# A hybrid RWKV, gMLP and expert block on one core: norm, modulation and gather edits, and the reversed values moved behind the receptance products

## The chip, the core and the metric

The kernel runs on one core of a Trainium2 chip. The core has a matrix engine (TensorE, PE in the profile), a vector engine (VectorE, DVE), a scalar engine (ScalarE, ACT) and a general engine (GpSimd, POOL), each with its own instruction stream; SyncE (SP) issues the DMAs. The engines share the on-chip memory (SBUF) and PE's accumulation banks (PSUM) and wait for each other on semaphores. The metric is the device time of one execution in microseconds (us), the median of several.

## The reference, cut to what matters

One layer over 512 latent and 256 context tokens, width 1024, float32:

```python
h = layer_norm(x) * (1 + sc1) + sh1          # context likewise
z = h @ w_in                                 # rwkv 3*1024 + 384, sgu 2*1024, gates 2*1024
# branch A: RWKV-7, forward and reverse
r, k, v, decays, kk, a = rwkv_prep(centred_shift(z_rwkv))
y_f, y_b = rwkv_scan(..., reverse=False), rwkv_scan(..., reverse=True)
bonus = sum(r * k * r_k, -1, keepdims=True) * v
y_a = (group_norm(y_f + y_b) * lnx_g + lnx_b + bonus) * g
# branch B: gating over chunks of 128 positions, 8 groups
u, v = split(gelu(z_sgu), 2)
v = layer_norm(v, sgu_ln_g, sgu_ln_b)
v = einsum('gpq,bnqgc->bnpgc', sgu_w, v) + sgu_b
y_s = u * v
x = layer_norm(ALPHA*x + gt1 * (merged(y_a, y_s) @ w_out), ln1_g, ln1_b)
# experts: 16, each takes its 64 best tokens
h = layer_norm(x) * (1 + sc2) + sh2
gate, idx = top_k(softmax(h @ router_w), 64)
ye = (silu(h[idx] @ w1) * (h[idx] @ w3)) @ w2 * gate
x = layer_norm(ALPHA*x + gt2 * segment_sum(ye, idx), ln2_g, ln2_b)
```

## The kernel before

The kernel is one program whose stages follow each other: loads, norm and transposes (to 50 us), the RWKV projections (to 316), the values of the gating branch (to 362), the gating branch and gates, with the preparation of the scan woven in (to 583), the scan (to 880), readout, output product and output norm (to 1004), router and top-k (to 1043), and the experts.

Projections. Every weight block is split into a high part `H` (ACT, line 159) and a rest `L` (line 160, on POOL or DVE) and PE multiplies with both: `zl` are products for the latent tokens, `zc` for the context. A loop runs over eight channel tiles `ct`, and its code is written by hand in the order in which each engine is to run it (`manual_schedule`). An iteration has the products for the keys (`z_k`, in two halves), the small products `b<-xp,wp` of decay and rate (`prep_a`, direction 0 or 1), the receptance (`z_r`) and the values (`z_v`). `shift_in` makes the shifted rows `kt`, `rt`, `vt` out of them: ACT starts each (line 351) and DVE adds two neighbours (lines 353 and 355, twice for a tile that has context). `prep_scan` on DVE is `g` (line 435) and a scan (line 437), then exponentials on ACT (442 to 444). `prep_vr` makes `vr` on ACT, the values with each 128 columns reversed; `prep_v` transposes `vt` and `vr` on PE (line 512) and copies the results to `vs` on ACT (line 513); `prep_bonus` is a product `bon<-rk,bones` on PE and `bo` on DVE (line 521). These three treat the tile of the iteration before (`ct - 1`).

The second tile of decay inputs, `pair_x`, is a copy of `dw` or `da` (ACT `xp`), its rest (DVE `xl`) and a DMA to the other half of the partitions.

Gating branch. Units run in a written list; `u` and `a`, `s`, `b` are products of the gating and gate columns. Ahead of them DVE normalises four tiles `vg` (line 1042), multiplies by the scale row and adds the bias row (lines 1043 and 1044). `ada_part` adds up the modulation (`adacc`, DVE line 567) and `ada_row` turns it into a row with products `adr` on PE.

Experts. `h2` is the normalised stream; POOL multiplies and adds the modulation rows (lines 1282 and 1283). The router does not read these but has the modulation in its columns. `gather` picks the tokens of two experts by products with one-hot columns `oh` and copies them to `xe` on ACT. The expert weights `we` come through 16 buffers.

## Time and profile before

| | us |
|---|---|
| median of three runs | 1998.64 (1995.78 to 1999.15) |
| the profiled execution | 1992.99 |
| its span, first to last instruction | 1991.0 |
| PE busy in the span | 1768.8 (89%) |
| DVE busy | 924.9 (46%) |
| ACT busy | 589.9 (30%) |
| POOL busy | 260.5 (13%) |

The busy times are those of the profiled execution, on one core, and add up stages with different limits. The profile's columns: a group of rows of a timeline gives the start, the busy time, the engine, the line of the kernel, the operation, the tiles written and read, how many instructions the row joins, and in brackets the idle time before it and what ended that.

### The profile page before, as it was taken

The page shows a single profiled execution, that of the slowest core. Times are in us where ns is not written, and L with a number is a line of the kernel's source. Part 1 is how long each engine was busy: PE and PEld are TensorE (multiplying, and loading weights), DVE is VectorE, ACT ScalarE, POOL GpSimd, SP SyncE. Part 2 cuts the span into 40 slices and gives each one's busy share as a digit, 9 for nine tenths or more (in the row PEclk, how much of TensorE's full clock was granted, in tenths as well). Part 3 has the DMA queues.
Part 4 walks back from the last instruction along what each step waited for, and adds up shares of the span by engine and source line. Part 5 has one row for each costly group of instructions (what it writes and reads, how often), then busy time and mean ns, then how long its engine had stood idle before and what let it go on. Part 6 is the DMA issues. An engine that isn't in the chain of part 4 may idle for free.

```text
span 1991.0 us, 32397 instructions
## 1 busy us (share of the span) xinstructions
PE 1768.8 (89%) x13248; PEld 1130.4 (57%) x13248; DVE 924.9 (46%) x1681; ACT 589.9 (30%) x1009; POOL 260.5 (13%) x207
## 2 busy tenths in 40 slices
PE   6999999899997979788959999899998899999895
PEld 3877778687777878677844434334343333434324
DVE  6689886688837768876970020010102002020115
ACT  2676775243246555343221111001011001011101
POOL 4422234010020100055520000000000000000000
PEclk9999999899999989898959999999999999999998
DMA  9365557567697667593289999999999999999995
GB/s 329 98 194 161 172 185 228 169 217 231 218 270 170 155 151 181 113 289 127 75 338 373 426 426 427 426 427 427 426 427 426 427 427 427 426 426 427 426 421 208
DMA packets 364011, 592.41 MB, mean 298 GB/s; under 512 B 220372, under 2 KB 282068, under 8 KB 315736
## 3 DMA queue, kind: packets, MB, share of 16 engines
q1 hardware_dynamic: 363864, 590.35, 80.3%
q8 instruction: 105, 1.72, 0.3%
q14 instruction: 42, 0.34, 0.1%
HBM read 541.78 MB, written 47.71 MB: 296 GB/s over the span
## 4 chain that ended last, share of the span: by engine, by line
DMA 41%; PE 8%; DVE 5%; issue 1%; POOL 0%; ACT 0%; DVEq 0%; SPq 0%; POOLq 0%; ACTq 0%
DMA we<-in_e 41%; PE hh L74 3%; PE yx L74 1%; PE co L74 1%; PE ye L74 1%; DVE x L1258 1%; PE lg L74 1%; PE xe L74 0%; DMA w<-in_wba 0%; DVE mt L1200 0%; DVE x L1266 0%; DVE mgL L1204 0%; PE hT L1518 0%; DVE wk L1436 0%; DVE m L1435 0%
## 5 line engine op out<-in xcount | busy, mean ns | idle before, releaser
L74 PE MATMUL hh<-we,xe 128*64 128x512 f32 x2048 | 462.3, 596 | 24.9 <-DMA we<-in_e 24.9
L74 PEld LDWEIGHTS hh<-we,xe 128*64 128x64 f32 x2048 | 149.5, 137 | 323.6 <-issue 261.0
L74 PE MATMUL ye<-we,hidT 128*64 128x512 f32 (+1 forms) x1216 | 254.0, 533 | 37.2 <-DMA we<-in_e 36.9
L1508 DVE TENSOR_TENSOR hd<-hd,hh 64x512 f32<-64x512 f32 x64 | 44.2, 690 | 518.7 <-ACT hd L1507 517.7
L74 PE MATMUL zl<-hL,H 128*128 128x512 f32 x816 | 261.6, 402 | 1.1 <-DVE hf L319 1.1
L74 PEld LDWEIGHTS ye<-we,hidT 128*64 128x64 f32 x1216 | 83.1, 136 | 200.1 <-DMA we<-in_e 105.3
L1507 ACT ACTIVATE hd<-hh 64x512 f32<-64x512 f32 x64 | 37.8, 590 | 490.9 <-PE hh L74 490.9
L74 PEld LDWEIGHTS zl<-hL,H 128*128 128x128 f32 x816 | 155.8, 193 | 30.2 <-issue 2.8
L74 PE MATMUL zl<-hL,L 128*128 128x512 f32 x408 | 163.5, 401 | 9.8 <-DVE L L160 9.8
L160 POOL TENSOR_TENSOR L<-w,H 128x1024 fp32r<-128x1024 f32 x54 | 138.4, 2571 | 206.0 <-ACT H L159 145.4
L1601 POOL TENSOR_TENSOR x<-x,row 128x1024 f32<-128x1024 f32 x2 | 4.6, 2338 | 941.5 <-DVE rv L129 941.5
L159 ACT ACTIVATE H<-w 128x1024 fp32r<-128x1024 f32 x91 | 94.9, 1053 | 87.2 <-PE zl L74 27.7
L1526 ACT ACTIVATE ye<-ye 64x512 f32<-64x512 f32 (+1 forms) x34 | 18.8, 553 | 271.5 <-PE ye L74 271.2
L1527 DVE SCALAR_TENSOR_TENSOR ye<-ye,gate,srow 64x512 f32<-64x512 f32 (+1 forms) x38 | 23.9, 664 | 147.7 <-ACT ye L1526 147.4
L74 PEld LDWEIGHTS zl<-hL,L 128*128 128x128 f32 x408 | 78.8, 193 | 21.8 <-DVE L L160 10.8
L716 DVE TENSOR_TENSOR tmpi<-Dt,Xt 128x31 f32<-128x31 f32 (+15 forms) x186 | 63.6, 342 | 14.6 <-DMA Dt<-Asd 8.9
L718 DVE TENSOR_TENSOR Xt<-Xt,tmpi 128x31 f32<-128x31 f32 (+15 forms) x186 | 63.8, 343 | 6.5
L74 PEld LDWEIGHTS xe<-oh,h 128*128 128x128 f32 x512 | 59.6, 196 | 8.9 <-issue 8.9
L74 PE MATMUL co<-ye,ohT 128*128 128x512 f32 (+1 forms) x144 | 62.7, 591 | 0.0
L74 PE MATMUL xe<-oh,h 128*128 128x128 f32 x512 | 61.8, 282 | 0.7 <-DVE oh L1459 0.7
L74 PEld LDWEIGHTS zc<-hC,H 128*128 128x128 f32 x288 | 54.0, 188 | 12.7 <-POOL hC L321 0.4
L160 DVE TENSOR_TENSOR L<-w,H 128x1024 fp32r<-128x1024 f32 x37 | 46.1, 1245 | 30.3 <-ACT H L159 28.7
(327 smaller groups left out, 2889.3 us busy)
## 6 DMA issues: line engine op xcount, KB each, us to landing
we<-in_e SPq DMA_DIRECT2D x376, 1024.0 KB, 19.6
w<-in_w_ch SPq DMA_DIRECT2D x51, 512.0 KB, 5.0
w<-in_ada_w SPq DMA_DIRECT2D x32, 512.0 KB, 5.3
xx<-Xkd SPq DMA_DIRECT2D x28, 512.0 KB, 5.6
adaw<-in_ada_w SPq DMA_DIRECT2D x16, 512.0 KB, 10.3
we<-in_e SPq DMA_DIRECT2D x32, 256.0 KB, 5.5
Xkd<-g SPq DMA_DIRECT2D x32, 192.0 KB, 2.7
Ald<-al SPq DMA_DIRECT2D x16, 384.0 KB, 2.3
```

The costliest lines, as they stand in the source:

```text
L74: PE.matmul(o, l, r, start=start, stop=stop, skip_group_check=True)
L159: S.activation(h, t, AF.Copy)
L160: (eng or G).tensor_tensor(l, t, h.bitcast(F32), OP.subtract)
L716: V.tensor_tensor(tv, Dt[:, j, None, j + 1:].to_broadcast([128, m, n]), X[:, 0:m, j:j + 1].to_broadcast([128, m, n]), OP.mult)
L718: V.tensor_tensor(X[:, 0:m, j + 1:], X[:, 0:m, j + 1:], tv, OP.subtract)
L1258: V.scalar_tensor_tensor(t[:, hs], R["x", i][:, hs], ALPHA, t[:, hs], op0=OP.mult, op1=OP.add)
L1507: S.activation(hd, pn[n][0:64], AF.Silu)
L1508: V.tensor_tensor(hd, hd, pn[n][64:128], OP.mult)
L1526: S.activation(y, p, AF.Copy)
L1527: V.scalar_tensor_tensor(y, p if same else y, gv[e - j][rs], gt2[rs, cs], op0=OP.mult, op1=OP.mult)
L1601: G.tensor_tensor(acc[i], acc[i], l2[0], OP.mult)
```

## The change

Five parts. `pair_x` makes tiles for the latent and the context columns apart (`xp`, `xl` and `xc`), with two copies where there was one. In the projection loop the copy `vr`, its transposes and copies, and the bonus product with `bo` stand around `z_r` in place of ahead of `prep_a`; the transposes of `vt` stay. In the gating branch the scale and bias of the norm are no longer applied to `vg`: the scale goes into the operation behind the product, and the bias into a tile `sbt` made of the sums of the gating weights (two products `cs`). `ada_row` is run once three more weight blocks have been split. The modulation of `h2` on POOL is gone, and `gather` applies it in its copies, one for each 128 columns. The diff, without the tables of columns and rows on the host's side and the reuse of a small tile:

```diff
@@ -292,16 +292,17 @@
             V.tensor_tensor(w[h], t[h], w[h].bitcast(F32), OP.subtract)
 
     def pair_x(t):
+        A, B = (T([128, 2, TL], n, F32R) for n in ("xp", "xl"))
+        Cc = T([128, 4, TC], "xc", F32R)
         hs = []
         for d in range(2):
             h, o = slice(64 * d, 64 * d + 64), slice(64 - 64 * d, 128 - 64 * d)
-            x2 = T([128, TT], "xp", F32R)
-            S.activation(x2[h], t[h], AF.Copy)
-            SY.dma_start(x2[o].bitcast(F32), x2[h].bitcast(F32))
-            lo = T([128, TT], "xl", F32R)
-            G.memset(lo[o].bitcast(F32), 0.0)
-            V.tensor_tensor(lo[h], t[h], x2[h].bitcast(F32), OP.subtract)
-            hs.append((x2, lo))
+            for x2, lo, ts in ((A[:, d], B[:, d], slice(TC, TT)), (Cc[:, d], Cc[:, 2 + d], slice(0, TC))):
+                S.activation(x2[h], t[h, ts], AF.Copy)
+                SY.dma_start(x2[o].bitcast(F32), x2[h].bitcast(F32))
+                G.memset(lo[o].bitcast(F32), 0.0)
+                V.tensor_tensor(lo[h], t[h, ts], x2[h].bitcast(F32), OP.subtract)
+            hs.append(((A[:, d], B[:, d]), (Cc[:, d], Cc[:, 2 + d])))
         return hs
 
     for k in range(KT):
@@ -413,10 +414,10 @@
         ev = s["ev", d] = []
         for o, lst, src, bias, off in (("g", w2p, dwt, "w0", TC), ("a", a2p, dat, "a0", 0)):
             p = P("b1")
-            w, (xh, xl) = lst[d][:, cs], src[d]
-            for o_, t_ in ((p, slice(TC, TT)), (p2[:, off:off + TC], slice(0, TC))):
-                mm(o_, w, xh[:, t_], True, False)
-                mm(o_, w, xl[:, t_], False, True)
+            w = lst[d][:, cs]
+            for o_, (xh, xl) in zip((p, p2[:, off:off + TC]), src[d]):
+                mm(o_, w, xh, True, False)
+                mm(o_, w, xl, False, True)
             ev.append((o, p, p2[:, off:off + TC], col(bias, d * 8 + ct)))
 
     def prep_tanh(ct, d):
@@ -500,10 +501,11 @@
         s = st_[ct]
         V.scalar_tensor_tensor(s["sq"], s["k"], col("k_k", ct), s["sq"], op0=OP.mult, op1=OP.mult)
 
-    def prep_v(ct):
+    def prep_v(ct, ds=(0, 1)):
         s = st_[ct]
         cs = slice(ct * 128, ct * 128 + 128)
-        for d, src in enumerate((s["v"], s.pop("vr"))):
+        for d in ds:
+            src = s.pop("vr") if d else s["v"]
             vs = T([128, 6, 128], "vs")
             for lo, n in ((0, 4), (4, 2)):
                 p = P("vT")
@@ -540,7 +542,6 @@
                      s["v"].rearrange("p (a b) -> p a b", b=128)[:, :, ::-1], AF.Copy)
 
     def prep_d1(ct):
-        prep_vr(ct)
         prep_scan(ct, 1)
         prep_kd(ct, 1)
         prep_akk(ct, 1)
@@ -568,7 +569,7 @@
         if k == 4 and wi < 3:
             ada_begin(wi + 1)
         if k == 7:
-            late["row"].append(a)
+            late["row"].append((zw.ns, a))
 
     zw.pre = -1
     with tc.manual_schedule():
@@ -581,8 +582,7 @@
             zw.step()
             z_k(ct, 1)
             if ct:
-                prep_v(ct - 1)
-                prep_bonus(ct - 1)
+                prep_v(ct - 1, (0,))
                 flush()
             prep_a(ct, 0)
             prep_tanh(ct, 0)
@@ -590,7 +590,12 @@
             prep_scan(ct, 0)
             prep_kd(ct, 0)
             zw.step()
+            if ct:
+                prep_vr(ct - 1)
             z_r(ct)
+            if ct:
+                prep_v(ct - 1, (1,))
+                prep_bonus(ct - 1)
             prep_k(ct)
             prep_rk(ct)
             prep_sg(ct, 0)
@@ -606,6 +611,7 @@
                 zw.step()
             prep_a(ct, 1)
             prep_tanh(ct, 1)
+        prep_vr(KT - 1)
         prep_d1(KT - 1)
         st_["ws"] = [zw.get(ZV + q) for q in range(4)]
         zw.eng = G
@@ -784,7 +790,7 @@
     Md = dp.tile([KT, 128, TL], F32, name="Md")
     Gd = dp.tile([KT, 128, TL], F32, name="Gd")
     def ada_row(wi):
-        a = late["row"].pop(0)
+        a = late["row"].pop(0)[1]
         m = T([128, D], "mod")
         for h in range(2):
             hs = slice(h * 512, h * 512 + 512)
@@ -931,10 +937,21 @@
                 else:
                     V.tensor_tensor(dst, dst, p[hs], OP.add)
 
-    sg_g, sg_b, sb_r = row(0), row(1), row(2)
+    sb_r = row(0)
     swt = T([128, 8, 128], "swt")
     SY.dma_start(swt, sgu_w)
+    sbt = T([128, 8, 128], "sbt")
     ug, gg_, late_mul = {}, {}, []
+
+    def sgu_bias():
+        for h in range(2):
+            p = P("cs")
+            mm(p, ones, swt[:, 4 * h:4 * h + 4, :])
+            for q in range(4):
+                g = 4 * h + q
+                V.scalar_tensor_tensor(sbt[:, g, :], p[:, q * 128:q * 128 + 128], col("sg_b", g),
+                                       sb_r[:, g * 128:g * 128 + 128], op0=OP.mult, op1=OP.add)
+
     ysH, ysL = [], []
     def u_z(g):
         pl, _ = zmm(zw.get(zi["u", g]), False)
@@ -946,8 +963,8 @@
         for i in range(4):
             mm(p[:, i * 128:i * 128 + 128], vg[i][:, g * 128:g * 128 + 128], swt[:, g, :])
         t = T([128, 4, 128], "sgt")
-        V.tensor_tensor(t, p.rearrange("p (a b) -> p a b", a=4),
-                        sb_r[:, None, g * 128:g * 128 + 128].to_broadcast([128, 4, 128]), OP.add)
+        V.scalar_tensor_tensor(t, p.rearrange("p (a b) -> p a b", a=4), col("sg_g", g),
+                               sbt[:, g, None, :].to_broadcast([128, 4, 128]), op0=OP.mult, op1=OP.add)
         u = ug.pop(g)
         V.tensor_mul(u, t.rearrange("p a b -> p (a b)"), u)
         if g % 2 == 0:
@@ -1034,20 +1051,20 @@
     zw.eng = V
     with tc.manual_schedule():
         hook("u", -1)
-        mv4 = cp.tile([128, 4, 2], F32, name="mv4")
+        mv4 = mv6[:, 0:4, :]
         for i in range(4):
             ln_stats(vg[i], mv4[:, i, :])
         r4 = rstd(mv4[:, :, 1], 4, LN_EPS)
         for i in range(4):
             V.tensor_scalar(vg[i], vg[i], mv4[:, i, 0:1], r4[:, i:i + 1], op0=OP.subtract, op1=OP.mult)
-            V.tensor_mul(vg[i], vg[i], sg_g)
-            V.tensor_add(vg[i], vg[i], sg_b)
         lag = []
         for t, j in UNITS:
             zw.eng = V
             run[t](j)
             if t == "u":
                 lag.append(j)
+                if j == 0:
+                    sgu_bias()
             if lag and (len(lag) > 2 or t != "u"):
                 u_s(lag.pop(0))
             if t == "s" and j == 0:
@@ -1058,9 +1075,11 @@
                 mul(*late_mul.pop(0))
             if t in "sa":
                 flush()
-            if late["row"]:
+            if late["row"] and late["row"][0][0] < zw.ns - 3:
                 ada_row(late["wi"])
                 late["wi"] += 1
+        if late["row"]:
+            ada_row(late["wi"])
         hook("end", 0)
 
     flush()
@@ -1279,8 +1298,6 @@
             t, h = acc[i], K([128, D], "h2")
             h2t[i] = h
             ln_apply(h, t, mv[:, q], rk[:, q:q + 1])
-            G.tensor_tensor(h, h, R["sc2"], OP.mult)
-            G.tensor_tensor(h, h, R["sh2"], OP.add)
             yield
 
     def router_cols():
@@ -1372,8 +1389,7 @@
     R["rw"] = K([128, KT, NE], "rw")
     SY.dma_start(R["rw"], rw)
     R["gt1"] = srow(Mo[0], K)
-    R["l1g"], R["l1b"] = row(3, K), row(4, K)
-    R["sh2"], R["sc2"] = srow(Mo[1], K), srow(Mo[2], K)
+    R["l1g"], R["l1b"] = row(1, K), row(2, K)
     affon = K([NE, 2, TL], "affT")
     affT, on16 = affon[:, 0], affon[:, 1]
     G.memset(on16, 1.0)
@@ -1466,7 +1482,9 @@
             for i in range(4):
                 mm(p[:, (k - k0) * 128:(k - k0) * 128 + 128], h2t[i][:, k * 128:k * 128 + 128], ohs[e0][:, i],
                    start=(i == 0), stop=(i == 3))
-        S.activation(xes[e0][:, k0:k1, :], p[:, :(k1 - k0) * 128].rearrange("p (a b) -> p a b", b=128), AF.Copy)
+        for k in range(k0, k1):
+            S.activation(xes[e0][:, k, :], p[:, (k - k0) * 128:(k - k0) * 128 + 128], AF.Identity,
+                         scale=R["s2c"][:, 1, k:k + 1], bias=R["s2c"][:, 0, k:k + 1])
 
     def route_back(e0):
         oh = ohs.pop(e0)
...
```

How the engines' streams change in an iteration of the loop (numbers behind a name tell tiles apart). ACT before, from `vr` of the previous tile, ahead of the exponentials `Ge` and `L` of direction 1, to the first `vs` copy:

```order
L539 ACTIVATE vr_1522<-vt_1442 128x768
L439 ACTIVATE kd_1527<-a_1469,omka,pcol 128x768
L442 ACTIVATE Ge_1529<-L_1525 128x12x64
L443 ACTIVATE L_1525<-L_1525 128x768
L444 ACTIVATE gC<-Ge_1529 128x12
L159 ACTIVATE H_1544<-w_1333 128x1024
L351 ACTIVATE kt_1548<-zc_1473,pcol 128x256
L351 ACTIVATE kt_1548<-zl_1472,pcol 128x512
L513 ACTIVATE vs_1555<-vT_1556 128x512
```

ACT after, later in the same iteration, from `kd` of direction 0 to the first table load:

```order
L440 ACTIVATE kd_1607<-a_1599,omka,pcol 128x768
L443 ACTIVATE Ge_1609<-L_1605 128x12x64
L444 ACTIVATE L_1605<-L_1605 128x768
L445 ACTIVATE gC<-Ge_1609 128x12
L159 ACTIVATE H_1617<-w_1463 128x1024
L541 ACTIVATE vr_1621<-vt_1456 128x768
L352 ACTIVATE rt_1648<-zl_1623,pcol 128x512
L515 ACTIVATE vs_1652<-vT_1653 128x512
L515 ACTIVATE vs_1652<-vT_1659 128x256
L497 ACT_TABLE_LOAD
```

`vr` no longer opens direction 1 of the previous tile; it stands behind the exponentials of direction 0, between a weight split `H` and `rt`, and two of the four `vs` copies follow `rt`.

DVE before, from the last key shift on:

```order
L355 SCALAR_TENSOR_TENSOR kt_1548<-zl_1472,pcol,kt_1548 128x511
L521 TENSOR_TENSOR bo_1579<-bon_1577,vt_1442 128x512
L435 TENSOR_SCALAR g_1601<-g_1601 128x768
L437 SCALAR_TENSOR_TENSOR L_1610<-rmask_98,g_1601 128x768
L448 TENSOR_TENSOR kd_1612<-kd_1612,kt_1548 128x768
L353 SCALAR_TENSOR_TENSOR rt_1651<-zl_1626,pcol,rt_1651 128x511
L355 SCALAR_TENSOR_TENSOR rt_1651<-zl_1626,pcol,rt_1651 128x511
L495 TENSOR_SCALAR sq_1607<-b_1656 128x256
```

DVE after, from the last key shift on:

```order
L356 SCALAR_TENSOR_TENSOR kt_1560<-zl_1486,pcol,kt_1560 128x511
L436 TENSOR_SCALAR g_1596<-g_1596 128x768
L438 SCALAR_TENSOR_TENSOR L_1605<-rmask_98,g_1596 128x768
L449 TENSOR_TENSOR kd_1607<-kd_1607,kt_1560 128x768
L354 SCALAR_TENSOR_TENSOR rt_1648<-zl_1623,pcol,rt_1648 128x511
L356 SCALAR_TENSOR_TENSOR rt_1648<-zl_1623,pcol,rt_1648 128x511
L523 TENSOR_TENSOR bo_1665<-bon_1663,vt_1456 128x512
L496 TENSOR_SCALAR sq_1602<-b_1668 128x256
L496 TENSOR_SCALAR sq_1602<-b_1667 128x512
```

`bo` moved from ahead of `g` and the scan to behind the two `rt` shifts, ahead of `sq`.

PE before, from behind `z_k` to the first products of `prep_a`:

```order
L512 MATMUL vT_1556<-ident,vt_1442 128x128 x4
L512 MATMUL vT_1562<-ident,vt_1442 128x128 x2
L512 MATMUL vT_1567<-ident,vr_1522 128x128 x4
L512 MATMUL vT_1573<-ident,vr_1522 128x128 x2
L74 MATMUL bon_1577<-rk_1376,bones 128x512
L74 MATMUL b_1591<-xp_513,wp_600 128x512
L74 MATMUL b_1591<-xl_516,wp_600 128x512
L74 MATMUL b_1590<-xp_513,wp_600 128x256
L74 MATMUL b_1590<-xl_516,wp_600 128x256
```

PE after, from the last products of `z_r` to the first of `z_v`:

```order
L74 MATMUL zl_1623<-hL_232,H_1330 128x512
L74 MATMUL zl_1623<-hL_228,L_1331 128x512
L514 MATMUL vT_1653<-ident,vr_1621 128x128 x4
L514 MATMUL vT_1659<-ident,vr_1621 128x128 x2
L74 MATMUL bon_1663<-rk_1388,bones 128x512
L74 MATMUL b_1667<-sq_1602,bones 128x512
L74 MATMUL b_1668<-sq_1602,bones 128x256
L74 MATMUL zl_1693<-hL_225,H_1465 128x512
```

The transposes of `vr` and the bonus product stood ahead of `prep_a` and now stand between `z_r` and the product `b<-sq` that leads to `z_v`.

## Rows read from the trace of the kernel before

**Rows 1.** The chain of work that ended last, by line, from the page.
```profile
DMA we<-in_e 41%; PE hh L74 3%; PE yx L74 1%; PE co L74 1%; PE ye L74 1%; DVE x L1258 1%; PE lg L74 1%; PE xe L74 0%; DMA w<-in_wba 0%; DVE mt L1200 0%; DVE x L1266 0%; DVE mgL L1204 0%; PE hT L1518 0%; DVE wk L1436 0%; DVE m L1435 0%
```
**Rows 2.** Stretches: length; busy PE, PEld, DVE, ACT, POOL; clock; DMA share; GB/s.
```profile
316.00:362.00 46.00, 46.00 (x210) 37.95 (x209) 20.42 (x27) 18.82 (x28) 23.72 (x17) 1.00 0.88 276
1096.00:1953.00 857.00, 794.95 (x3804) 321.24 (x3800) 109.20 (x186) 83.86 (x142) 0.00 (x0) 0.99 1.01 425
```
**Rows 3.** Waits of PE in the projections (total us, times, longest).
```profile
PE b L74 <- ACT vs L513: 16.9, 7, 3.3
```
**Rows 4.** Table of stretches, six iterations of the projection loop, columns as in rows 2.
```profile
110.80:302.10 191.30, 177.66 (x926) 147.55 (x925) 164.32 (x187) 134.32 (x205) 51.32 (x31) 0.97 0.58 176
```
**Rows 5.** Waits of DVE in these six iterations, columns as in rows 3.
```profile
DVE rt L353 <- ACT rt L351: 15.4, 6, 2.6
```
**Rows 6.** Timeline of DVE, one iteration (start, us, what).
```profile
173.74 0.68 DVE L521 TENSOR_TENSOR bo<-bon,vt 128x512 f32<-128x512 f32 x1
...
180.10 0.75 DVE L353 SCALAR_TENSOR_TENSOR rt<-zl,pcol,rt 128x511 f32<-128x511 f32 x1 [2.58 <-ACT rt L351]
...
188.44 3.17 DVE L487 SCALAR_TENSOR_TENSOR L<-L,a 128x768 f32<-128x768 f32 x1
191.53 0.47 DVE L353 SCALAR_TENSOR_TENSOR vt<-zc,pcol,vt 128x255 f32<-128x255 f32 x1
```
**Rows 7.** Timeline of ACT, same iteration.
```profile
162.09 0.85 ACT L539 ACTIVATE vr<-vt 128x768 f32<-128x768 f32 x1 [4.61 <-DVE vt L355]
...
179.39 0.67 ACT L351 ACTIVATE rt<-zl,pcol 128x512 f32<-128x512 f32 x1
...
186.27 0.47 ACT L351 ACTIVATE vt<-zc,pcol 128x256 f32<-128x256 f32 x1 [0.67 <-PE zc L74]
```
**Rows 8.** Timeline of PE, same iteration.
```profile
164.08 0.82 PE L512 MATMUL vT<-ident,vr 128*128 128x128 f32 x6
164.73 1.02 PE L74 MATMUL bon<-rk,bones 128*128 128x512 f32 x2
...
168.66 0.58 PE L74 MATMUL b<-xp,wp 128*128 128x256 f32 x1 [2.45 <-ACT vs L513]
...
176.62 1.45 PE L74 MATMUL b<-sq,bones 128*128 128x512 f32 x4
```
**Rows 9.** Timeline of POOL; two lines of DVE (ns: least, median, most).
```profile
188.40 2.39 POOL L160 TENSOR_TENSOR L<-w,H 128x1024 fp32r<-128x1024 f32 x1 [6.42 <-DMA Xkd<-g]
...
L435 DVE TENSOR_SCALAR g<-g x15: 548/551/1561, 78.4 to 302.7; 128x768 f32<-128x768 f32 x15
...
L487 DVE SCALAR_TENSOR_TENSOR L<-L,a x15: 951/3001/3170, 93.5 to 316.9; 128x768 f32<-128x768 f32 x15
```
**Rows 10.** Table of stretches, behind two waits of PE, columns as in rows 2.
```profile
168.40:171.90 3.50, 3.24 (x10) 2.76 (x11) 3.43 (x4) 2.94 (x8) 1.38 (x2) 0.51 0.29 112
381.50:387.00 5.50, 5.50 (x13) 4.34 (x14) 4.59 (x4) 0.00 (x0) 0.00 (x0) 0.51 0.01 3
```
**Rows 11.** Timelines of DVE and PE, gating norm.
```profile
366.88 1.22 DVE L1043 TENSOR_TENSOR vg<-vg,row 128x1024 f32<-128x1024 f32 x1
...
380.21 1.22 DVE L160 TENSOR_TENSOR L<-w,H 128x1024 fp32r<-128x1024 f32 x1
...
381.49 0.80 PE L74 MATMUL zl<-hL,L 128*128 128x512 f32 x1 [8.15 <-DVE L L160]
```
**Rows 12.** Timeline of PE, branch b.
```profile
529.09 2.67 PE L74 MATMUL adr<-adacc,ones 128*128 128x512 f32 x4 [3.23 <-DVE adacc L567]
```
**Rows 13.** Timelines of DVE, POOL and PE, output norm to router.
```profile
949.96 1.28 DVE L1258 SCALAR_TENSOR_TENSOR x<-srow,x 128x512 f32<-128x512 f32 x2
...
985.58 2.40 POOL L1282 TENSOR_TENSOR h<-h,srow 128x1024 f32<-128x1024 f32 x1 [3.49 <-ACT h L146]
...
985.79 5.54 DVE L1258 SCALAR_TENSOR_TENSOR x<-srow,x 128x512 f32<-128x512 f32 x2
...
1004.14 6.98 PE L74 MATMUL lg<-rw,h2T 128*128 128x16 f32 x32 [2.40 <-DVE rt L135]
```

More of the change, by code (lines that the diff above doesn't have):

```diff
@@ L36 @@
 for _k, _w in (("w0", 16), ("a0", 16), ("k_k", 8), ("k_a", 8), ("lnx_g", 8), ("lnx_b", 8), ("r_k", 8),
[L37 removed]
+               ("shift", 81), ("ada_b", 16), ("ln1_g", 8), ("ln1_b", 8), ("sg_g", 8), ("sg_b", 8)):
     PC[_k] = _n
@@ L1569, in block_kernel @@
             ohT.pop(e - 2), yes.pop(e - 2), gv.pop(e - 2)
-    l2 = row(5, K), row(6, K)
+    l2 = row(3, K), row(4, K)
     fst = K([128, 4, 4, 6], "fst")
@@ L1593, in block_kernel @@
     with tc.manual_schedule():
-        mv = cp.tile([128, 4, 2], F32, name="mvf")
+        mv = mv6[:, 0:4, :]
         for i in (1, 3, 0, 2):
@@ L1631, in _layout @@
         pcols(g["lnx_b"][0]), pcols(g["r_k"][0]), pcols(sw), pcols(ada_b[:2048]),
-        pcols(g["ln1_g"][0]), pcols(g["ln1_b"][0])], axis=1)
+        pcols(g["ln1_g"][0]), pcols(g["ln1_b"][0]), pcols(g["sgu_ln_g"][0]), pcols(g["sgu_ln_b"][0])], axis=1)
     return {
@@ L1639, in _layout @@
         "pc": pc,
-        "rows": np.stack([g["sgu_ln_g"][0], g["sgu_ln_b"][0], g["sgu_b"][0].reshape(-1), g["ln1_g"][0],
-                          g["ln1_b"][0], g["ln2_g"][0], g["ln2_b"][0]]),
+        "rows": np.stack([g["sgu_b"][0].reshape(-1), g["ln1_g"][0], g["ln1_b"][0], g["ln2_g"][0], g["ln2_b"][0]]),
         "w_ch": blocks(w_ch),
```

1 line of the change is left out of this document (removed).

## Prediction

> **What bounds the kernel now.** I read the page's chain first, because it says what the end hangs on. 41% of it is one entry, the DMA of expert weights [rows 1]. The table by stage shows when that holds: from 1096 to 1953 us the DMA share is 1.01, while VectorE (DVE) is busy 109.20 of 857 us and ScalarE (ACT) 83.86 [rows 2]. The weights fill their 16 buffers ahead of time and then wait for the first expert matmuls to release them. So the stream's length is fixed and its start is not: whatever is saved or lost on the path before the first expert moves the end by as much, and whatever is saved inside the stream moves nothing.
>
> Before the stream the stages follow each other, each with its own limit. In the projections I asked for the waits of TensorE (PE): it waits 7 times, 16.9 us in all, at the products `b<-xp` for a copy by ACT of line 513 [rows 3]. That looks like the limit, but DVE is busy 164.32 of the 191.30 us of six iterations, and its own wait comes back every time: for ACT's `rt`, 6 times, 15.4 us [rows 4, 5]. I follow one iteration and call K the time at which the four `kt` shifts on DVE end; here K = 173.74, where `bo` starts. DVE: `bo`, `g`, scan, `kd`, a wait for `rt` until K+6.36, two `rt` shifts, `sq`, six more operations, `L` of L487, then `vt` at K+17.79 [rows 6]. PE has finished z_v at K+12.5 by then (ACT's `vt`, which waits for it, starts at 186.27 [rows 7]); PE stalls 2.45 us in an iteration [rows 8] and is still ahead. The period, 191.30 / 6 = 31.9 us [rows 4], is that of the loop DVE to ACT to DVE. After z_v of the last iteration this reverses: in 316 to 362 us PE is busy 46.00 of 46.00 us [rows 2], so a PE that comes late there stays late.
>
> **The change part by part.**
>
> *`pair_x` in two widths.* ACT copies 512 and 256 columns where it copied 768. The `vt` and `rt` rows show .47 for 256 and .67 for 512, `vr` .85 for 768 [rows 7]: .29 more for each of two copies on the path of `da`, at most .6, and at least 0 since operations overlap when they follow closely. I take +0.3.
>
> *`vr`, its transposes and the bonus behind z_r.* What this removes: the wait of 2.45 and its like, on an engine that is ahead. I count 0 for that. What it adds, at full clock:
> - `bo` leaves the place ahead of the scan; its row says .68, of which .6 counts (the next operation starts before the last has ended, as all rows of DVE and ACT show here). The scan ends .6 earlier, and ACT's exponentials with it. ACT would start `rt` at K+5.05 (before 179.39, K+5.65). Now `vr` stands there, .85, of which .75 counts: `rt` starts at K+5.8, .15 later than now, and DVE's `rt` at K+6.5. Before, ACT ran `vr` after 4.61 us of idleness [rows 7], free of charge.
> - `bo` comes after the two `rt` shifts, .6, so DVE's queue from `sq` on is .75 late.
> - PE now waits for `vr` (K+5.05+.85 = K+5.9), transposes .65 (164.08 to 164.73), bonus product .5 (half of the 1.02 of two), `b<-sq` 1.1 of its 1.45 [rows 8], and z_v starts at K+8.15. Its length is 186.27 less 176.62 less the 1.1, 8.55, so it ends at K+16.7, 4.2 later than before.
> - DVE's `vt` cannot start before ACT's, some K+17.2, which is no later than now. But the split `L` on POOL follows z_v too: POOL took 188.40 to 190.79 [rows 9], K+14.66, and moves by 4.2, to K+18.9 till K+21.3. Today it blocks L487, which takes 3.17 there [rows 6] and between .95 and 3.17 in its 15 runs, half of them over 3.0. L487, .75 late, is then over before it. It would now meet `g` (L435) at K+19.6, after the four `vt` shifts (2.4 by the rows of .47 to .75); that operation takes .55 in the median of 15 and 1.56 in one [rows 9], so it can be stretched. So the 2.2 won at L487 turns into about 1.7 lost at `g`: the next K comes at 17.2, plus what lies between `vt` and K now (31.9 - 17.8 = 14.1), plus 1.7, 33.0 against 31.9.
> - The clock. After the stall of 2.45 PE runs 3.5 us at .51, 1.2 GHz [rows 10]. In the new order PE works 177.66 / 6 = 29.6 us per iteration, of which a mean clock of .97 [rows 4] cost .95 and the parts just listed take 10.8. So 17.85 lie between z_v and the end of z_r, which comes near K+16.7+1.6+17.85-34.6 = K+1.5 (1.6 and 34.6 as below), and PE idles to K+5.9, 4.4 us, longer than that stall. The transposes, bonus and `b<-sq` then run at half clock: up to 3.5/2 = 1.75 more; I take 1.6, which shifts all behind it.
>
> The page "TensorE: Matmul & The Clock Gate" of the Trainium skill, section "What's actually happening", states that the throttled clock is the default and activity releases it; it speaks against a gap placed ahead of work that others wait for. The trace agrees (.51 behind the stall); by the rule alone no other sum follows.
>
> Six periods of 1.1 + 1.6 (33.0 + 1.6 = 34.6 each) and the lag of PE at the end, 4.2 + 1.6, give 22; not every iteration will meet POOL twice, so I take **+21**. Bounds: +1 without the second meeting and without the clock, 6 x (-.6) + 4.2; +11 with the meeting and full clock; +24 with 1.75 and another stretched operation.
>
> *Gating norm without its scale and bias.* Eight DVE operations of 1.22 go (the `vg` row at 366.88). Behind them stands the weight split `L` at 380.21, for which PE waits 8.15 us, and then PE runs 5.5 us at .51 [rows 10, 11]. With 8 x 1.22 = 9.8 gone `L` is ready at 371.6 and PE wants it at 381.49 less 8.15, 373.3, so the wait (8.15) and the half clock (2.75) go. Two new `ones` products, .5 each by the bonus row, cost 1.0. Eight small additions of 128 columns lie behind that `L`, in DVE's idle time while PE runs the next unit; without that cover they would cost at most 8 x .68 (the `bo` row [rows 6]). Sum -9.9, taken as **-10**, between -9 and -11. *The modulation row* taken three weight steps later ends PE's wait of 3.23 for `adacc` [rows 12], and part of the half clock behind it: **-3.9**, between 0 (DVE is nearly full there, and the next split may take the wait's place) and -4.4.
>
> *Modulation of the router's input, off POOL.* Four POOL operations of 2.4 go in 985 to 997. Beside them two `x` operations of DVE took 5.54, while the same pair took 1.28 at 949.96; that DVE chain ends in the `rt` for which PE's router product waits 2.40 [rows 13]. The wait and a good part of PE's earlier one go, but then h2T and its copies limit: **-3.4**, between -1 and -8. The four later POOL operations lie beside the top-k on DVE: 0.
>
> The page "SBUF — State Buffer" of the Trainium skill, section "SBUF: two separate sides", states that DVE and GpSimd share one port pair as an exclusive lock, held for a whole instruction by whichever starts first. The 5.54 against 1.28 and the 3.17 against .95 agree.
>
> *The gather's copies* into 128 columns with scale and bias run under the stream, where ACT is busy a tenth of the time [rows 2]: 0. If the first of them delayed the release, 8 copies would cost under 1.
>
> **Sum.** .3 + 21 - 10 - 3.9 - 3.4 = +4.0. The profiled execution took 1992.99 us (span 1991.0 and 2 around it), so 1997.0 by it; the median of the three runs is 5.65 above it, and I forecast against the median: 1998.64 + 4 = **2002.6 us**.
>
> **The rivals.**
> 1. *The loop meets POOL less.* Faster. If POOL's split slips past `g` and the gap does not cost clock, the projections lose only 1: .3 + 1 - 17.3 = -16, 1982.6 us; with the meeting and full clock (+11), -6, 1992.6. For it: the meeting hangs on 1.6 us. Against: the stall of 2.45 was followed by half clock, and the gap is longer. It wins from a loss below 13 in the projections. Chance .20.
> 2. *PE's stall is the limit after all.* Then 16.9 and the 5.7 that a mean clock of .97 cost come back: -22.6 - 17 = -40, 1959 us. For it: PE is at 177.66 of 191.30 [rows 4]. Against: DVE's wait for `rt` recurs in all iterations, and z_v is over 5 us ahead. Chance .08.
> 3. *The gains are given back.* Slower than forecast: projections +24, DVE full at the modulation row (0), the gating norm -9, the router -1, `pair_x` .6: +14.6, 2013 us. For it: DVE's queue fills the place of any wait removed on PE. Chance .22.
> 4. *The order does nothing*, because `vr` is hidden in ACT's wait for the scan wherever it stands: projections 0, sum -17, 1982. Against: after the change `vr` is issued behind the scan's exponentials, not ahead of them. It goes with rival 1 in time and in chance.
>
> **How the numbers follow.** The forecast has .50, spread from 1995 to 2009. A measurement here tells 0.2%, 4 us, from no change. Of the .50, .06 lie below -4, .21 within 4 and .23 above; with the rivals: faster .06 + .19 + .08 = .33, same .22, slower .45. The range takes rival 1 whole and rival 3 to its end: 1983 to 2014; rival 2 and the tails outside hold under .2.
>
> **What the profile will show.** Right: PE's wait for ACT `vs` gone, a wait of 4 to 5 us at `vT<-ident,vr` for ACT's `vr` in each of seven iterations with half clock behind it, six periods of 34 to 35, L487 at .95 and L435 stretched; no wait at 373, `adr` without one; `x` of L1258 at 1.3 for two, router product some 3 us nearer to the out product. Wrong: periods of 31 to 32 (rival 1), of 28 to 30 (rival 2), or new waits for `L` behind 373 and 526 (rival 3).

## The result, and the profile after

The changed kernel takes 2011.57 us in the median (2007.58 to 2012.75, four runs) against 1998.47 of the kernel before (1995.78 to 1999.15): a ratio of 1.0072, 95% interval 1.0052 to 1.0092. It is slower, by 13.1 us, where 4.0 were forecast. The profiled execution has a span of 2009.8 us against 1991.0, 18.8 more; the steps below are counted in these two executions.

The table shows where the same instruction starts in the two traces, how much later it starts in the changed kernel, how much of that arose since the row above, and what the forecast gave for the same stretch.

| start of | before | after | later by | of it in this stretch | forecast |
|---|---|---|---|---|---|
| K of the second tile (end of the `kt` shifts) | 110.9 | 109.7 | -1.2 | -1.2 | +0.3 |
| K of the last tile | 302.2 | 326.4 | +24.2 | +25.4 | +16.2 |
| gating norm on DVE | 366.03 | 397.23 | +31.2 | +7.0 | +5.8 |
| first gating product `sgu` | 389.13 | 411.13 | +22.0 | -9.2 | -10 |
| last product of branch b | 537.78 | 554.19 | +16.4 | -5.6 | -3.9 |
| first scan product `zp` | 587.10 | 611.09 | +24.0 | +7.6 | 0 |
| last output product `yx` | 995.0 | 1020.8 | +25.8 | +1.8 | 0 |
| gather `xe` | 1039.52 | 1058.05 | +18.5 | -7.3 | -3.4 |

(The forecast's 22 in the projections is entered by its parts, 6 x 2.7 and 5.8; it was then rounded to 21.) From the gather on both kernels take the same time.

The chain of work that ended last, of the changed kernel, still has the expert weights as its largest entry [rows 1]:

```profile
DMA we<-in_e 36%; PE hh L74 5%; PE ye L74 2%; PE yx L74 2%; PE co L74 1%; PE xe L74 1%; PE hT L1536 1%; PE lg L74 0%; DVE wk L1452 0%; DVE m L1451 0%; DVE x L1277 0%; PE h2T L1323 0%; DVE mt L1219 0%; DVE x L1625 0%; DVE mgL L1223 0%
```

The table of stretches for the six iterations, the two stretches around one wait of PE, and the expert stream (length; busy PE, PEld, DVE, ACT, POOL; clock; DMA share; GB/s):

```profile
109.70:326.40 216.70, 185.51 (x924) 151.42 (x924) 167.58 (x187) 135.51 (x205) 47.33 (x31) 0.92 0.52 156
147.00:150.60 3.60, 0.00 (x0) 0.00 (x0) 0.87 (x2) 3.46 (x6) 0.63 (x1) 0.83 0.54 146
150.60:154.20 3.60, 3.52 (x9) 2.35 (x10) 1.73 (x3) 2.75 (x5) 1.73 (x1) 0.50 0.16 49
1096.00:1953.00 857.00, 796.83 (x3754) 319.85 (x3752) 110.43 (x191) 96.32 (x184) 0.00 (x0) 0.99 1.01 427
```

Six periods take 216.70 us where they took 191.30 [rows 4]: 36.1 each. DVE is busy 167.58 of them and PE 185.51, 3.3 and 7.9 more than before, so most of the 25.4 is waiting. The clock fell from .97 to .92; the third row shows it at .50, the lower of its two levels (1.2 GHz), in the 3.6 us behind PE's wait.

The waits of PE in the projections and of DVE in the six iterations (total us, times, longest), of the changed kernel:

```profile
PE vT L514 <- ACT vr L541: 41.1, 7, 10.0
...
DVE rt L354 <- ACT rt L352: 20.2, 6, 3.4
DVE sq L496 <- PE b L74: 7.6, 6, 1.9
DVE bo L523 <- PE bon L74: 7.2, 6, 1.2
DVE sq L502 <- ACT sq L498: 5.7, 6, 0.9
DVE vt L354 <- ACT vt L352: 5.4, 6, 0.9
```

PE's wait for the `vs` copies [rows 3] is gone, and a wait for `vr` of 41.1 us has come in its place. DVE waits longer for `rt` [rows 5], and for three things that it never waited for: the bonus product, `b<-sq` and `vt`. The longer waits for `rt` (4.8) and the three new ones (7.2, 7.6 and 5.4) add up to 25.0 us, nearly all that six periods lost.

One iteration, in the timelines of PE, ACT, POOL and DVE; K is 144.81 here. (The two rows of PE at 190 us are from the next iteration.)

```profile
150.68 1.54 PE L514 MATMUL vT<-ident,vr 128*128 128x128 f32 x6 [4.86 <-ACT vr L541]
152.01 1.91 PE L74 MATMUL bon<-rk,bones 128*128 128x512 f32 x2
153.72 2.71 PE L74 MATMUL b<-sq,bones 128*128 128x512 f32 x4
155.93 0.96 PE L74 MATMUL zl<-hL,H 128*128 128x512 f32 x2
...
190.04 1.62 PE L74 MATMUL b<-sq,bones 128*128 128x512 f32 x4
191.31 0.81 PE L74 MATMUL zl<-hL,H 128*128 128x512 f32 x2
...
149.80 0.83 ACT L541 ACTIVATE vr<-vt 128x768 f32<-128x768 f32 x1
150.53 0.67 ACT L352 ACTIVATE rt<-zl,pcol 128x512 f32<-128x512 f32 x1
...
164.70 0.47 ACT L352 ACTIVATE vt<-zc,pcol 128x256 f32<-128x256 f32 x1 [4.17 <-PE zc L74]
...
166.78 2.42 POOL L160 TENSOR_TENSOR L<-w,H 128x1024 fp32r<-128x1024 f32 x1 [14.45 <-ACT H L159]
...
151.23 0.75 DVE L354 SCALAR_TENSOR_TENSOR rt<-zl,pcol,rt 128x511 f32<-128x511 f32 x1 [3.37 <-ACT rt L352]
...
153.97 0.69 DVE L523 TENSOR_TENSOR bo<-bon,vt 128x512 f32<-128x512 f32 x1 [1.20 <-PE bon L74]
156.47 1.02 DVE L496 TENSOR_SCALAR sq<-b 128x256 f32<-128x256 f32 x2 [1.81 <-PE b L74]
...
163.36 0.95 DVE L488 SCALAR_TENSOR_TENSOR L<-L,a 128x768 f32<-128x768 f32 x1
165.21 0.48 DVE L354 SCALAR_TENSOR_TENSOR vt<-zc,pcol,vt 128x255 f32<-128x255 f32 x1 [0.89 <-ACT vt L352]
...
167.68 1.99 DVE L436 TENSOR_SCALAR g<-g 128x768 f32<-128x768 f32 x1
```

PE stands still for 4.86 us until `vr` (149.80, K+5.0) is written; of its seven waits the first is 9.97 us and the last 6.88, and the five between are 4.8 to 4.9. The transposes then take 1.33 us, the bonus product 1.71 (152.01 to 153.72) and `b<-sq` 2.2 (153.72 to 155.93, where z_v begins), all at half clock. At full clock, in half_zr_twice below, the same three take .71, .86 and 1.1. The six iterations are not alike: in three, as here, `b<-sq` takes 2.2 and the period is 36.3, 36.4 and, for the last, 38.4; in the other three the transposes and the bonus product are as slow, but the clock comes back during `b<-sq`, which takes 1.1 to 1.3 (the rows at 190 us), and the period is 35.1 to 35.3. DVE follows each: `bo` at K+9.2, `sq` at K+11.7. `vt` waits for z_v (K+20.4), L488 (which was L487) takes .95 where it was blocked [rows 6], and `g` is stretched to 1.99 by the split on POOL that began .9 earlier.

### The profile page after: what moved, and what is told of

It is laid out like the page before. It is cut to its first block, busy times and chain, and to the rows that moved or that the text cites. A ratio compares the mean times of both kernels' runs of the same rounds, so it can differ in the third digit from the quotient of the medians.

```text
span 2009.8 us, 32487 instructions
## 1 busy us (share of the span) xinstructions
PE 1770.3 (88%) x13252; PEld 1129.0 (56%) x13252; DVE 917.4 (46%) x1685; ACT 605.5 (30%) x1058; POOL 234.7 (12%) x203
## 4 chain that ended last, share of the span: by engine, by line
DMA 36%; PE 12%; DVE 3%; issue 0%; ACT 0%; DVEq 0%; SPq 0%
DMA we<-in_e 36%; PE hh L74 5%; PE ye L74 2%; PE yx L74 2%; PE co L74 1%; PE xe L74 1%; PE hT L1536 1%; PE lg L74 0%; DVE wk L1452 0%; DVE m L1451 0%; DVE x L1277 0%; PE h2T L1323 0%; DVE mt L1219 0%; DVE x L1625 0%; DVE mgL L1223 0%
## 5 line engine op out<-in xcount | busy, mean ns | idle before, releaser
L160 POOL TENSOR_TENSOR L<-w,H 128x1024 fp32r<-128x1024 f32 x54 | 133.9, 2487 | 272.4 <-ACT H L159 238.8
## 6 DMA issues: line engine op xcount, KB each, us to landing
adaw<-in_ada_w SPq DMA_DIRECT2D x16, 512.0 KB, 10.3
```

Source lines behind the costliest of these rows:

```text
L160: (eng or G).tensor_tensor(l, t, h.bitcast(F32), OP.subtract)
```

## The experiments

All times are medians of 4 to 12 runs; each ratio compares with runs of the kernel before on the same chip, whose median lay between 1994.4 and 1997.0.

| kernel | median us | before | ratio, 95% interval |
|---|---|---|---|
| order_undone | 1988.01 | 1995.38 | 0.9962 (0.9949 to 0.9976) |
| order_only | 2026.17 | 1995.38 | 1.0161 (1.0144 to 1.0177) |
| vr_behind_zv | 1980.46 | 1995.38 | 0.9920 (0.9905 to 0.9934) |
| half_zr_twice | 2000.01 | 1995.38 | 1.0023 (1.0013 to 1.0032) |
| row_at_once | 1981.73 | 1996.08 | 0.9931 (0.9914 to 0.9949) |
| vr_behind_rt | 1975.37 | 1996.08 | 0.9898 (0.9879 to 0.9916) |
| norm_only | 2007.79 | 1996.08 | 1.0058 (1.0043 to 1.0074) |
| gather_only | 1988.57 | 1996.08 | 0.9969 (0.9953 to 0.9984) |
| vr_early | 1979.15 | 1996.99 | 0.9909 (0.9894 to 0.9924) |
| norm_rows5 | 2008.04 | 1996.99 | 1.0053 (1.0040 to 1.0066) |
| first_load_free | 1979.65 | 1996.99 | 0.9909 (0.9896 to 0.9923) |
| norm_load_free | 2009.14 | 1994.37 | 1.0069 (1.0055 to 1.0083) |

**Is it the order, and which part of it?** The theory: PE's wait for `vr`, ahead of a product that DVE waits for, with half clock behind it. The rivals: the other four parts cost the time; `bo` and the longer queue on DVE cost it.

*order_undone*, against the changed kernel:

```diff
-                prep_v(ct - 1, (0,))
+                prep_v(ct - 1)
+                prep_bonus(ct - 1)
...
-            if ct:
-                prep_vr(ct - 1)
             z_r(ct)
-            if ct:
-                prep_v(ct - 1, (1,))
-                prep_bonus(ct - 1)
...
     def prep_d1(ct):
+        prep_vr(ct)
...
```

> The changed kernel with the projection loop as before (the copy vr, its transposes and the bonus product at their old places); the other four parts stay. If the projection order costs what the traces show (the gating norm starts 31.2 us later than before, of which pair_x gives back 1.2), the time is some 32 us below the changed kernel, about 1980, 18 below the kernel before. If gains made upstream are swallowed by the loads of the gate weights (a wait of PE on the weight split at 585 us in the changed kernel), about 1985 to 1990. If the other parts cost the time and not the order, over 2000.

It is faster than the kernel before, but by 7.4 us, not 18. That is the time of the second case expected, but not by its cause, since the loss lies behind the gather (below). Its periods are those of before (111.0 to 302.2 for six), so the order cost all of the loss in the loop. In its trace the gather stands at 1023.9, 15.6 earlier than before, and 9 of these are gone at the end; that is taken up below.

*order_only*, against the kernel before:

```diff
-                prep_v(ct - 1)
-                prep_bonus(ct - 1)
+                prep_v(ct - 1, (0,))
                 flush()
...
+            if ct:
+                prep_vr(ct - 1)
             z_r(ct)
+            if ct:
+                prep_v(ct - 1, (1,))
+                prep_bonus(ct - 1)
...
     def prep_d1(ct):
-        prep_vr(ct)
...
```

> The kernel before with the projection order of the change and nothing else. If the order costs 32 us: about 2030. If a part of its lag is taken up by the wait of 8.15 us for the gating norm (PE comes late, the norm does not): 2022. If the forecast's price of 21 was right and something else cost the rest: about 2020.

30.8 us slower, nearest to the first of the three. Six periods take 216.7 here too, and the gating norm starts 33.3 us later; nothing takes up the lag, and PE's wait for the norm's split is there as before, 8.1 us.

*vr_behind_zv*, against the changed kernel:

```diff
-                prep_v(ct - 1, (1,))
-                prep_bonus(ct - 1)
...
             z_v(ct)
+            if ct:
+                prep_v(ct - 1, (1,))
+                prep_bonus(ct - 1)
```

> The changed kernel, but the transposes of vr and the bonus product (with their vs copies and bo) behind z_v in place of ahead of the product b<-sq; the copy vr on ACT stays ahead of rt. If PE's wait for vr, standing ahead of b<-sq, is the cost: that wait and the half clock behind it go, the period falls back to about 32 us and the time to 1980 to 1987. If ACT's queue is the cost (vr ahead of rt, .15 by the forecast) or bo on DVE, it stays above 2000.

1980.5: PE's wait was the cost. The copy `vr` is where the change put it, ahead of `rt`, and DVE's wait for `rt` is as long as in the changed kernel, but nothing waits for `vr` any more and six periods take 190.2.

*vr_early*, against the changed kernel: only the copy goes back.

```diff
-            if ct:
-                prep_vr(ct - 1)
             z_r(ct)
...
     def prep_d1(ct):
+        prep_vr(ct)
...
```

> The changed kernel with only the copy vr back at its place ahead of direction 1 on ACT; its transposes and the bonus product stay behind the receptance products. Should the copy's place be the cause (PE waits for vr, 41 us in seven waits): PE finds vr done, the wait shrinks to the one for the square of the keys, and the time is that of vr_behind_zv or order_undone, 1977 to 1988. Should the place of the transposes and the bonus be the cause: 2000 or more.

1979.2, some 32 us below the changed kernel. So the place of one copy of .85 us, behind the exponentials of direction 0 in ACT's queue in place of ACT's idle time, made the loss, together with PE's products that wait for it (moving these away, in vr_behind_zv, mends it as well). By themselves the transposes and the bonus product cost nothing at their new place. The table of stretches for six iterations, the timelines of ACT and of PE, and PE's wait in the projections, of vr_early:

```profile
110.30:302.50 192.20, 175.92 (x924) 145.76 (x924) 169.01 (x187) 133.62 (x205) 51.53 (x31) 0.98 0.58 175
...
162.63 0.85 ACT L541 ACTIVATE vr<-vt 128x768 f32<-128x768 f32 x1 [3.85 <-issue]
...
172.24 0.82 PE L514 MATMUL vT<-ident,vr 128*128 128x128 f32 x6
172.90 1.02 PE L74 MATMUL bon<-rk,bones 128*128 128x512 f32 x2
...
PE b L74 <- ACT sq L402: 19.9, 7, 3.6
```

`vr` again follows 3.85 us of idleness on ACT, PE's transposes of it start without a wait, and the clock is .98. PE now waits 19.9 us in the projections for another operation of ACT, `sq`, more than the 16.9 that it waited for the `vs` copies before [rows 3], and yet the period is that of before (32.0 against 31.9). This wait of PE costs nothing.

*half_zr_twice*, against the changed kernel:

```diff
-        st_[ct]["r"] = shifted(4 + 3 * ct, False, "rt")
+        st_[ct]["r"] = shifted(4 + 3 * ct, False, "rt", 4)
...
+        for k in range(twice):
+            hh, hlo = hl(k)
+            mm(pl, wh[:, k, :], hh, k == 0, False)
+            mm(pl, wh[:, k, :], hlo, False, False)
+            mm(pl, wl[:, k, :], hh, False, False)
         for k in range(KT):
```

> The changed kernel with the first half of each receptance product computed twice (the second pass overwrites the first, the result is the same): 2.7 us more of PE work per iteration, put into PE's wait ahead of the transposes of vr. If half clock behind the wait is what the forecast priced too low: the wait falls from 4.9 to some 2.2 us, PE stays at full clock, and each of six iterations wins about 3 us, the time is about 1990. If waiting as such is the cost: as the changed kernel, 2011, within 3 us. If PE is the bound: 2011 + 19 = 2030.

More work for PE made the kernel faster, by 11.6 us against the changed kernel's median (2000.0 against 2011.6; 9.8 by the two ratios). The table of stretches and two waits, of half_zr_twice:

```profile
108.90:315.40 206.50, 193.74 (x1005) 160.75 (x1005) 167.01 (x187) 135.38 (x205) 47.66 (x31) 0.98 0.54 163
...
148.29 0.88 PE L519 MATMUL vT<-ident,vr 128*128 128x128 f32 x6 [2.12 <-ACT vr L546]
149.00 1.02 PE L74 MATMUL bon<-rk,bones 128*128 128x512 f32 x2
149.86 1.45 PE L74 MATMUL b<-sq,bones 128*128 128x512 f32 x4
...
181.84 1.54 PE L519 MATMUL vT<-ident,vr 128*128 128x128 f32 x6 [2.11 <-ACT vr L546]
```

The wait is 2.1 to 2.2 in all six iterations, the mean clock .98, and six periods take 206.5, 34.4 each, against 36.1. In four iterations, as at 148.29, the clock stays full behind the wait, the bonus product takes .86 and the period is 33.5 or 33.6, which is 1.6 to 2.9 us less than in the changed kernel at the same place. In the third and the last, after a wait of the same length, the transposes and the bonus product run at half clock again (1.54 for the transposes at 181.84, where .88 stood at 148.29), and the periods are 35.2 and 37.3; what decides between the two is not shown here. So where the clock is kept it is worth nearly the 3 us expected. The time of 2000 lies above the 1990 expected in part because two iterations of six did not keep it. What is left, 33.5 against 31.9, stays because z_v still starts late: `vr` still comes at K+5.

*vr_behind_rt*, against vr_behind_zv:

```diff
-            if ct:
-                prep_vr(ct - 1)
             z_r(ct)
+            if ct:
+                prep_vr(ct - 1)
```

> The kernel vr_behind_zv with the copy vr on ACT behind rt in place of ahead of it. The copy is wanted only behind z_v there. If DVE's wait for ACT's rt sets the loop, as the forecast had it, each of six periods loses the .75 us of the copy: 4.5 us, about 1976. If a stretched operation behind a POOL split takes it back: the same as vr_behind_zv, within 2 us.

1975.4, the fastest of all, 20.7 us below the kernel before. Six periods take 185.7 in place of 190.2, .75 less each, as much as the forecast counted for the copy on ACT: with PE's wait for `vr` out of the way the loop is what the forecast said, DVE to ACT to DVE.

**Where did the other parts' gain go?** They were to give 17 and gave 7.4 in order_undone.

*row_at_once*, against vr_behind_zv:

```diff
-            if late["row"] and late["row"][0][0] < zw.ns - 3:
+            if late["row"]:
```

> The kernel vr_behind_zv with the modulation rows made as soon as their sums are there, as before, in place of three weight steps later. In the traces the delay wins some 5 us up to the last product of branch b and loses it again at a wait for a weight split 30 us later. If so, the time is that of vr_behind_zv within 2 us. If the forecast's 3.9 us were real to the end, 1984 to 1986.

1981.7 against 1980.5: the delay of the modulation row is worth 1.3 us by the medians (2.2 by the two ratios, whose intervals overlap), so no gain is shown at the end. In the traces the first scan product follows the second tile's K by 467.9 us without the delay and by 468.4 with it. The waits of PE in the gating stage, first of row_at_once, then of vr_behind_zv:

```profile
PE adr L74 <- DVE adacc L568: 3.2, 1, 3.2
PE zl L74 <- DVE L L160: 1.9, 1, 1.9
```

```profile
PE zl L74 <- DVE L L160: 2.6, 2, 2.1
PE zl L74 <- ACT H L159: 1.9, 1, 1.9
```

The wait for `adacc` (3.2) goes, and waits for the weight split `H` (1.9, for a load) and one more for `L` take its place. In the changed kernel they stand at 585.73 (2.19 us) with half clock behind them:

```profile
585.73 0.74 PE L74 MATMUL zl<-hL,H 128*128 128x512 f32 x2 [2.19 <-ACT H L159]
...
583.00:586.00 3.00, 0.81 (x4) 0.39 (x3) 0.29 (x1) 1.38 (x2) 0.00 (x0) 1.00 1.02 403
586.00:592.30 6.30, 5.78 (x15) 4.18 (x15) 5.27 (x6) 1.22 (x2) 0.00 (x0) 0.52 1.01 320
```

The DMA share around it is 1.02 and 1.01: PE had come early to a stretch in which the loads were full already.

*gather_only*, against the kernel before (the rows `sh2` and `sc2` are no longer loaded):

```diff
-            G.tensor_tensor(h, h, R["sc2"], OP.mult)
-            G.tensor_tensor(h, h, R["sh2"], OP.add)
...
-        S.activation(xes[e0][:, k0:k1, :], p[:, :(k1 - k0) * 128].rearrange("p (a b) -> p a b", b=128), AF.Copy)
+        for k in range(k0, k1):
+            S.activation(xes[e0][:, k, :], p[:, (k - k0) * 128:(k - k0) * 128 + 128], AF.Identity,
+                         scale=R["s2c"][:, 1, k:k + 1], bias=R["s2c"][:, 0, k:k + 1])
```

> The kernel before without the modulation of h2 on POOL and with scale and bias in the gather's copies, nothing else. Forecast: 3.4 us; the trace of the changed kernel shows 6.8 between the last output product and the gather: 1988.5 to 1992. If the first expert weight load then waits for a later release, as it does in order_undone (1003 us, 18 us behind the last output product), nothing is left of it: 1995.

7.5 us faster by the medians, 6.2 by the ratio. The timelines of DVE and PE at the output norm, of the changed kernel, which answer to [rows 13]:

```profile
1011.58 1.28 DVE L1277 SCALAR_TENSOR_TENSOR x<-srow,x 128x512 f32<-128x512 f32 x2
...
1023.43 1.86 PE L74 MATMUL lg<-rw,h2T 128*128 128x16 f32 x16
...
1026.04 3.64 PE L74 MATMUL lg<-rw,h2T 128*128 128x16 f32 x32
```

The two `x` operations take 1.28 in place of 5.54. The first 16 router products take 1.86 in both kernels; the 32 that took 6.98 behind a wait of 2.40, at a granted clock of .50 (1004.1 to 1011.0), now follow without a wait and take 3.64 at full clock (1.00 from 1025.3 to 1030.0). In gather_only itself they follow without a wait, too, and take 5.31.

*norm_only*, against the kernel before (with `sgu_bias` and the operation behind the product as in the change):

```diff
-            V.tensor_mul(vg[i], vg[i], sg_g)
-            V.tensor_add(vg[i], vg[i], sg_b)
...
+                if j == 0:
+                    sgu_bias()
```

> The kernel before with the gating norm's scale and bias folded and nothing else. The forecast's price is 10 us: the wait of 8.15 us and the half clock behind it go, about 1986. If the loads of the gate weights, or the first expert weight load, take it back: 1990 to 1995.

11.7 us slower, though the norm's own stretch is shorter by the 9.2 that the changed kernel shows (366.5 to 380.4, 13.9 us where the kernel before needs 23.1). All of it was lost again, and more, in two places: the first scan product is 6.7 earlier than before, the first readout product 1.6 and the gather not at all; and behind the gather the expert weights came at 421 GB/s, so that the gather is followed by 963.6 us in place of 951.5. What takes the norm's gain ahead of the gather is not shown. The stretch 1130 to 1900, of norm_only, and then of gather_only:

```profile
1130.00:1900.00 770.00, 702.06 (x3299) 285.78 (x3299) 95.84 (x166) 74.79 (x126) 0.00 (x0) 1.00 1.01 421
```

```profile
1130.00:1900.00 770.00, 713.52 (x3316) 284.98 (x3314) 100.28 (x172) 83.26 (x159) 0.00 (x0) 0.99 1.01 427
```

*norm_rows5*, against norm_only, the unused rows of an input dropped:

```diff
-    sb_r = row(2)
+    sb_r = row(0)
...
-    R["l1g"], R["l1b"] = row(3, K), row(4, K)
+    R["l1g"], R["l1b"] = row(1, K), row(2, K)
...
-    l2 = row(5, K), row(6, K)
+    l2 = row(3, K), row(4, K)
```

> norm_only with the rows input cut to the five rows that are read, as in the changed kernel; the program is otherwise the same. In norm_only the expert weights came at 421 GB/s, in all other runs at 427, which is 11 us over the stream. If the place of the inputs in memory sets that: 427 and some 1992 to 1996. If the program itself does (its buffers, its order of loads): 421 and 2007 as norm_only.

421 GB/s and 2008.0 again. It isn't the size of that input.

*first_load_free*, against order_undone:

```diff
+    V.memset(T([128, 1024], "pad")[:, 0:8], 0.0)
...
     last = out_ln(1, (1,), ps)
```

(the line added four times)

> order_undone with four small unused tiles (a store of zeros to each) ahead of the router's last half, which moves the router's tiles to other places, so that the first expert weight loads no longer wait for the router's last products. In order_undone the first load waits until 1003 us and nothing moves for some 18 us ahead of it. If that wait is where order_undone loses 9 us behind the gather: about 1979. If something else holds the stream up: 1988 as order_undone.

1979.7, which is 8.4 us below order_undone by the medians and 10.6 by the two ratios, about the 9 that order_undone had lost. The waits of the load queue SP and the stretch 990 to 1000, of order_undone:

```profile
SPq L1465 <- DVE x L1273: 22.0, 1, 22.0
SPq L1465 <- PE lg L74: 15.2, 1, 15.2
...
990.00:1000.00 10.00, 7.91 (x46) 7.53 (x44) 6.25 (x28) 2.05 (x4) 0.00 (x0) 0.58 0.00 0
```

and the same stretch of first_load_free:

```profile
990.00:1000.00 10.00, 7.91 (x62) 7.54 (x61) 7.49 (x34) 2.20 (x5) 0.00 (x0) 0.77 0.90 362
```

In order_undone the first weight load stands ahead of all others in SP's queue and waits 22.0 us for an `x` of DVE and then 15.2 for the router's products `lg`, since its buffer was last a tile of the router; nothing moves meanwhile (share 0.00). So the stream starts late and its start, not the gather, sets the end. The four unused tiles move the router's tiles elsewhere: in first_load_free the first load still waits 22.0 us for `x`, but not for `lg` behind it, and goes out at 989.77 in place of 1003.08.

*norm_load_free*, against norm_only, the same line four times at the same place:

```diff
+    V.memset(T([128, 1024], "pad")[:, 0:8], 0.0)
...
     last = out_ln(1, (1,), ps)
```

(the line added four times)

> norm_only with the four unused tiles of first_load_free, so that the third expert weight load no longer waits for the router's products (14.6 us in norm_only). If the late load and the lower rate of 421 GB/s hang on which buffers the loads find free: 427 GB/s and 1984 to 1990, the norm's own gain. If only the late load goes and the rate stays: some 2000. If neither matters: 2008.

2009.1, with 421 GB/s. But the edit did not do here what it was made for: the load queue still waits for the router's products. Its waits for them, of norm_only and then of norm_load_free:

```profile
SPq L1464 <- PE lg L74: 20.0, 2, 14.6
```

```profile
SPq L1468 <- PE lg L74: 20.6, 1, 20.6
```

So this run doesn't settle what the late load costs. That the late load isn't what lowers the rate is seen elsewhere: in these three programs (norm_only, norm_rows5, norm_load_free) the loads `adaw`, which are issued in the first 25 us, already need 10.8 us to land where they need 10.2 to 10.3 in all the others. Nor is it the norm's edit by itself, since the changed kernel and seven others have that edit too and run at 427, nor the chip, since norm_only ran on the same chip as gather_only, and norm_rows5 on that of vr_early. Why these three load all their data a little slower stays open. So norm_only doesn't tell what the norm's edit is worth alone.

## Why the prediction was right, and where it fell short

**The direction and the steps.** The step that decided was right: PE's wait was not the limit and its removal gave nothing. In vr_early PE waits longer than before, for another operation, and the period is the same, and in vr_behind_rt .75 us less on ACT ahead of `rt` shortens each period by .75. `vr` at K+5.0 with PE's wait of 4.86 (forecast 4.4), half clock behind it, L488 at .95 and a stretched `g` all stand in the trace. vr_early and vr_behind_zv show that it is the copy's place together with the products that wait for it. Rival 1 (POOL missed, clock kept) and rival 2 (PE is the limit) are refuted by the periods of 35 to 38; rival 4 (`vr` hidden) by PE's seven waits. One step beside these was off without effect: DVE's queue was to be .75 late behind `bo`, but L488 starts at K+18.6, some 4 us late, since `bo` and `sq` wait for PE; `vt` waits .9 for ACT behind it even so.

**The term that was too small** is the price of the projections: +21, with +24 as its bound; it measured 25.4 + 7.0 = 32.4. Its working took the bonus product as .5, half of a row that joins two. But the two instructions of that row are one product (`b<-sq`, two products, is x4): half_zr_twice has it at .86 from its start to the next, and the changed kernel, at half clock, at 1.71. The half clock was taken as 1.6 in each period: against the 2.67 us that the three products take at full clock it cost 2.6 in three iterations and 1.5 to 1.7 in the three others. So z_v starts at K+11.2 in three and at K+10.1 to K+10.3 in three, where the forecast had K+9.75 (8.15 and 1.6): that is 5.6 of the 9.1 us that six periods missed (36.1 against 34.6 each). Another 2.1 belong to the last period, in which 17.9 us lie between DVE's `vt` and the next K in place of the 15.8 forecast (15.9 in the other five); the rest is a few tenths in each between the start of z_v and `vt`. The lag of PE at the end measured 7.0 against 5.8; there, too, z_v starts 1.2 later than forecast (K+11.0).

**The modulation row's -3.9** was real for 30 us and then given back: 5.6 by the last product of branch b, nothing at the scan. This is what the lower end of that term named (the next split may take the wait's place), and the term should have stood there. Rival 3 had it so, and rival 3's time, 2013, is the nearest; its norm at -9 held, too (-9.2), but its projections at +24 and its router at -1 did not (32.4 and -7.3), so that its time is near because two errors cancel.

**The router's -3.4** was too careful: 7.3 from the last output product to the gather. I counted only the wait of PE (2.40 and part of an earlier one); the clock gave 3.3 more, 3.64 in place of 6.98 for 32 router products.

**The gating norm's -10** measured -9.2 at its place; its two new products were priced by the same row, at .5 each, where a product of this shape takes .86. Its worth by the end of the program is not shown, since norm_only was held up by its slower loads. **The gather's copies** cost nothing: from the gather to the end the changed kernel takes 951.7 us of span and the kernel before 951.5.

**The premise** that whatever is saved ahead of the stream moves the end by as much holds for the changed kernel by these two numbers, but not in general: in order_undone 15.6 us saved up to the gather left 6.5 of span, since the first load waited for its buffer.

**The basis.** In the profiled executions the change costs 18.8, in the medians 13.1; single runs of the kernel before spread over as much as 10 us here (1990.47 to 2000.58 in one set of 13). The forecast's error is about 9 by the medians. By them the time lies inside the range, 2.4 us below its upper end; the 18.8 of the two traces is more than the range allowed (15.4 above 1998.64). So that the range held owes something to luck: the projections alone cost 11 more than forecast, and the basis was a median 5.65 above the traced execution.

## What to carry to other kernels

Before an operation is moved, see what its engine was doing at the old place and what stands behind it at the new one: a copy of .85 us that ran in 4 us of idleness cost 32 us when it was put where another engine waits for it, ahead of a product that a third engine needs; with either of the two elsewhere the loss was gone. When a wait vanishes, look for the next resource that is already full (the loads at 585 us), and for a load whose buffer comes free late, since one such load holds the whole queue. A wait of one engine is worth its length only when that engine sets the period: in vr_early PE waits 19.9 us and loses nothing by it, and in half_zr_twice 2.7 us of useless products in each iteration, put into PE's wait, made the changed kernel faster.
